# Feed-forward products of a diffusion trunk: which accumulators share a PSUM tile, when the sums of u are formed, and when the conditioning products run

## The chip, the cores and the metric

The kernel runs on one core of a Trainium2 chip. Five engines work from their own in-order instruction queues: PE (TensorE, matrix products into PSUM), DVE (VectorE), ACT (ScalarE), POOL (GpSimd) and SP (SyncE, which here only issues DMAs). An instruction that needs another engine's result waits on a semaphore, and everything behind it in the same queue waits with it. The metric is the device time of one execution in microseconds (us).

## The reference, cut to what matters

There are 512 latent tokens and 256 context tokens, 1024 features wide, in 6 tiles of 128 tokens. Two layers each do a half-step SwiGLU, a token mixer (differential attention in layer 0, grouped-query attention in layer 1) and another half-step SwiGLU; all in float32.

```python
D_MODEL, SEQ, CTX_LEN, DEPTH, N_MOD, D_FF = 1024, 512, 256, 2, 9, 2816

def swiglu(h, w_in, w_out):
    gate, up = jnp.split(h @ w_in, 2, axis=-1)
    return (jax.nn.silu(gate) * up) @ w_out

def adaln(cond, w, b):
    m = jax.nn.silu(cond) @ w + b
    return m.reshape(m.shape[:-1] + (N_MOD, D_MODEL))

def modulated_norm(h, g, m, k):
    return rmsnorm(h, g) * (1.0 + m[..., k + 1, :]) + m[..., k, :]

def half_ffn(h, m, k, g_pre, g_post, w_in, w_out):
    y = swiglu(modulated_norm(h, g_pre, m, k), w_in, w_out)
    return h + 0.5 * m[..., k + 2, :] * rmsnorm(y, g_post)

for i in range(DEPTH):
    ctx_out = i < DEPTH - 1
    m, mc = adaln(c, ada_w[i], ada_b[i]), adaln(c_ctx, ada_w[i], ada_b[i])
    h, hc = (half_ffn(x, mod, 0, g[0], g[1], ffn_w_in[i, 0], ffn_w_out[i, 0]) for x, mod in ((h, m), (hc, mc)))
    ...  # token mixer of the layer; in the last layer the context is only read
    h = half_ffn(h, m, 6, g[4], g[5], ffn_w_in[i, 1], ffn_w_out[i, 1])
    if ctx_out:
        hc = half_ffn(hc, mc, 6, g[4], g[5], ffn_w_in[i, 1], ffn_w_out[i, 1])
```

Each layer has nine modulation vectors v = 0..8 (shift, scale, gate of three sub-layers) for two conditions, that of the latent tokens and that of the context tokens. In the last layer the context tokens are not used after the mixer has read them, so v = 5..8 of layer 1 are wanted for the latent condition alone.

## The kernel before, in words

`trunk` runs six stages one after the other: `ffn` for (layer, half) = (0, 0), `diff_attention`, `ffn` (0, 1), `ffn` (1, 0), `grouped_attention`, `ffn` (1, 1). The first three `ffn` stages work on all six token tiles (384 columns in each of two halves), the last on the four latent tiles (256 columns).

Every float32 operand is split into a rounded high part and a low remainder (`split`, L103 the high part on ACT, L104 the low part on DVE), and a product is three matmuls: high by high, high by low, low by high.

An `ffn` stage has these parts.

* **Direct chunks.** A chunk is 128 columns of `gate` and the same 128 of `up`. Chunk 0 (and chunk 1 in the last stage) is multiplied as it stands, pair of token tiles by pair (`mms`, L459), as soon as a pair's normalised input u is finished (`need`). Where all six tiles are at work, chunk 1 follows as 96 matmuls from L713.
* **Sums of u.** `uh`, `ul` hold u by halves. The kernel then forms four sums of quarters of u, t1, t2, t3 and t4 (L538, L539, L543, L544, L549, L550), in `sums_first` to `sums_fourth`, after the direct chunk 0.
* **Seven-product chunks.** The other 20 chunks use a scheme of Winograd's that needs seven products of half the depth in place of eight (`chunk`, with `product` at L604). Each of the seven products is 12 matmuls. I number them in their order in the queue: 1 (`pa`, g1), 2 (`pc`, s1), 3 (`pb`, s2), 4 (`pd`, s3), 5 (`pa` again, g2), 6 (`pc` again, s4), 7 (`pd` again, u2). `pa` and `pc` are the two banks of one PSUM tile x (`bank2`), `pb` and `pd` are tiles of one bank each.
* **What a chunk does beside PE.** ACT copies `pa` into c1 (L620), `pc` into c5 (L623), applies Silu to `pa` (L633) and to a sum (L637). DVE adds z2 = pb + c1 (L626, the *first add*), z3 = pd + z2 (L629, the *second add*), pc + z2 (L636, the *third add*), pd + z2 (L642) and multiplies (L643). POOL adds z3 + c5 (L630) and multiplies (L640). `keep` stores the chunk's result by DMA.
* **Operands of the next chunk** are made during the chunk (`Operands.steps`): four POOL sums of weight halves (L579 to L582, the *POOL sums*), three high parts on ACT and three low parts on DVE of 1024 columns (gate before the first add, two more after the second add), and one of 512 columns (u2) after the third add.
* **Fillers.** The modulation vectors of later stages are computed in the shadow of this: `ada` loads 512 KB of `ada_w` eight times and DVE multiplies and accumulates it for each of the two conditions (L168, L172, the *acc* instructions); PE then adds over partitions (L188, 16 short matmul records), and DVE adds bias and gain. One `ada` is 10 steps, eight of them with acc instructions. `Fillers.fill` is called twice in a chunk, after the first add (*filler one*) and before the last add L642 (*filler two*), and runs as many steps as are due.
* **Output.** `w_out` multiplies by `ffn_w_out` in groups of chunks given by `GROUPS`, and `w_out_last` finishes the tokens and begins the next stage's input (`Finish`).

In `chunk` the order on PE, DVE, ACT and POOL is the written one (`tc.manual_schedule`); outside, a scheduler sets it by readiness and priority. A writer of a tile waits for the earlier readers of that tile, and the unit is the whole tile: product 2 writes the other bank of x and still waits for the copy of `pa`.

## Time and profile before

| | us |
|---|---|
| median of 3 runs | 2971.38 (2970.94 to 2972.20) |
| profiled execution, its own time | 2967.32 |
| its span | 2965.5 |
| PE busy | 2691.8 (91%) |
| DVE busy | 2194.3 (74%) |
| ACT busy, POOL busy | 1190.7 (40%), 1160.7 (39%) |

The median is 4.06 us above the profiled execution. A row of the timeline gives start, duration, engine, line, operation, what is written and read, and in brackets how long the engine had waited and for what. The mean granted clock of TensorE was 0.975 of full speed.

### The profile page before, as it was taken

How to read it: one execution, taken by the hardware profiler on the slowest of the kernel's cores; microseconds unless marked ns; L12 is line 12 of the kernel's file. 1: busy time of each engine (PE TensorE's matmuls, PEld its weight loads, DVE VectorE, ACT ScalarE, POOL GpSimd, SP SyncE). 2: the span in 40 equal slices, each digit the busy share in tenths (PEclk: the TensorE clock that was granted, in tenths of full speed). 3: DMA queues.
4: the chain of work that ended last, by engine and by line, in shares of the span. 5: the costliest groups of instructions: out<-in, count | busy, mean ns of one | idle time of the engine just before them, and what ended most of it. 6: DMA issues, size and time to landing. Idle time of an engine off the chain costs nothing.

```text
span 2965.5 us, 41112 instructions
## 1 busy us (share of the span) xinstructions
PE 2691.8 (91%) x15472; PEld 2441.9 (82%) x15472; DVE 2194.3 (74%) x2894; ACT 1190.7 (40%) x2427; POOL 1160.7 (39%) x1145
## 2 busy tenths in 40 slices
PE   7888989989999988999999989999998999688898
PEld 5878877878999977888878788888887997677777
DVE  4977878566777787977875678888857778666664
ACT  4322323245666565333342333333414555433342
POOL 1655640044333345655600456564005211465601
PEclk9999999999999989999999999999999999899999
DMA  7344447331101123443473234444734112333362
GB/s 226 113 130 138 143 135 255 122 107 54 44 30 46 50 71 99 137 128 119 137 236 122 96 102 133 146 139 139 239 111 142 44 51 65 100 114 111 111 222 88
DMA packets 302176, 355.33 MB, mean 120 GB/s; under 512 B 15848, under 2 KB 234136, under 8 KB 301976
## 3 DMA queue, kind: packets, MB, share of 16 engines
q1 hardware_dynamic: 301976, 352.69, 37.5%
q8 instruction: 122, 2.00, 0.3%
q14 instruction: 78, 0.64, 0.1%
HBM read 304.10 MB, written 48.55 MB: 119 GB/s over the span
## 4 chain that ended last, share of the span: by engine, by line
PE 61%; DVE 16%; issue 9%; ACT 8%; POOL 4%; DMA 2%; SPq 0%; ACTq 0%; DVEq 0%; POOLq 0%
PE y_ps L404 21%; PE ff_ps L604 15%; PE ff_p L604 9%; PE qkv_ps L755 5%; DVE acc L172 4%; DVE wl L104 3%; PE ff_ps L459 2%; PE S L933 1%; ACT wh L103 1%; PE o_ps L1005 1%; DVE h L363 1%; ACT sil L633 1%; ACT y L250 1%; ACT one L620 1%; DVE t L539 1%
## 5 line engine op out<-in xcount | busy, mean ns | idle before, releaser
L404 PE MATMUL y_ps<-wh,gx 128*128 128x512 f32 x1936 | 606.3, 392 | 9.3 <-ACT wh L103 8.0
L404 PEld LDWEIGHTS y_ps<-wh,gx 128*128 128x128 f32 x1936 | 364.4, 188 | 88.9 <-ACT wh L103 10.1
L604 PE MATMUL ff_ps<-uh,wh 128*128 128x384 f32 (+1 forms) x960 | 323.2, 337 | 102.0 <-ACT sil L633 75.5
L104 DVE TENSOR_TENSOR wl<-stage,wh 128x1024 fp32r<-128x1024 f32 x204 | 309.7, 1521 | 121.7 <-ACT wh L103 121.4
L404 PE MATMUL y_ps<-wl,gx 128*128 128x512 f32 x968 | 379.2, 392 | 2.7 <-DVE wl L104 2.6
L172 DVE SCALAR_TENSOR_TENSOR acc<-stage,scond,acc 128x1024 f32<-128x1024 f32 x224 | 359.1, 1642 | 0.3 <-DMA stage<-in_ada_w 0.3
L395 DVE TENSOR_TENSOR y<-y_ps,y 128x512 f32<-128x512 f32 x324 | 222.2, 687 | 154.5 <-PE y_ps L404 153.7
L103 ACT CAST wh<-stage 128x1024 fp32r<-128x1024 f32 x204 | 211.8, 1052 | 272.8 <-PE y_ps L404 239.5
L604 PE MATMUL ff_ps<-uh,wl 128*128 128x384 f32 (+1 forms) x960 | 314.9, 328 | 4.4 <-DVE wl L104 4.4
L604 PE MATMUL ff_ps<-ul,wh 128*128 128x384 f32 (+1 forms) x960 | 314.1, 327 | 0.0
L604 PE MATMUL ff_p<-t,wh 128*128 128x384 f32 (+1 forms) x1280 | 305.7, 324 | 0.0
L350 POOL TENSOR_TENSOR yg<-y,g 128x512 f32<-128x512 f32 x44 | 59.2, 1346 | 592.7 <-DVE y L395 590.5
L604 PEld LDWEIGHTS ff_ps<-uh,wh 128*128 128x128 f32 x960 | 185.4, 193 | 126.4 <-ACT sil L633 98.7
L630 POOL TENSOR_TENSOR g<-two,one 128x384 f32<-128x384 f32 (+1 forms) x80 | 141.5, 1768 | 313.6 <-issue 108.9
L104 DVE TENSOR_TENSOR wl<-raw,wh 128x1024 fp32r<-128x1024 f32 x160 | 222.6, 1412 | 48.0 <-ACT wh L103 47.9
L604 PEld LDWEIGHTS ff_p<-t,wh 128*128 128x128 f32 x1280 | 225.2, 191 | 3.7 <-issue 3.7
L103 ACT CAST wh<-raw 128x1024 fp32r<-128x1024 f32 x160 | 167.0, 1046 | 149.3 <-POOL raw L582 149.3
L404 PEld LDWEIGHTS y_ps<-wl,gx 128*128 128x128 f32 x968 | 182.6, 189 | 43.8 <-DVE wl L104 7.0
L604 PE MATMUL ff_ps<-t,wh 128*128 128x384 f32 (+1 forms) x640 | 162.5, 339 | 51.3 <-ACT one L620 51.3
L604 PE MATMUL ff_p<-t,wl 128*128 128x384 f32 (+1 forms) x640 | 206.8, 323 | 0.0
L604 PEld LDWEIGHTS ff_ps<-uh,wl 128*128 128x128 f32 x960 | 185.9, 194 | 5.8 <-DVE wl L104 5.8
L604 PEld LDWEIGHTS ff_ps<-ul,wh 128*128 128x128 f32 x960 | 186.0, 194 | 0.0
(237 smaller groups left out, 6518.2 us busy)
## 6 DMA issues: line engine op xcount, KB each, us to landing
stage<-in_ffn_w_in SPq DMA_DIRECT2D x176, 512.0 KB
stage<-in_ada_w SPq DMA_DIRECT2D x136, 512.0 KB
stage<-in_ffn_w_out SPq DMA_DIRECT2D x88, 512.0 KB
gd<-g SPq DMA_DIRECT2D x66, 384.0 KB
gr<-gd SPq DMA_DIRECT2D x60, 384.0 KB
stage<-in_da_w_in SPq DMA_DIRECT2D x64, 192.0 KB
hd<-h SPq DMA_DIRECT2D x18, 512.0 KB
h<-hd SPq DMA_DIRECT2D x16, 512.0 KB
```

Source lines behind the costliest of these rows:

```text
L103: nc.scalar.copy(hi, src)
L104: nc.vector.tensor_tensor(out=lo, in0=src, in1=raw(hi), op=ALU.subtract)
L172: nc.vector.scalar_tensor_tensor(out=acc[c], in0=st, scalar=scond[:, k, c : c + 1], in1=acc[c], op0=ALU.mult, op1=ALU.add)
L250: nc.scalar.activation(junk, src, AF.Square, accum_out=ss)
L350: nc.gpsimd.tensor_tensor(out=self.yg[:, cols], in0=ys[t][:, cols], in1=self.gate[1 if t < CT else 0][:, cols], op=ALU.mult)
L363: nc.vector.scalar_tensor_tensor(out=h, in0=yg, scalar=r, in1=h, op0=ALU.mult, op1=ALU.add)
L395: nc.vector.tensor_tensor(out=y, in0=ps, in1=y, op=ALU.add)
L404: nc.tensor.matmul(ps, lhsT=x, rhs=w, start=(i == 0), stop=(i == n - 1))
L459: nc.tensor.matmul(ps, lhsT=ww[:, k, :], rhs=moving(uu, k, two), start=(k == 0 and n == 0), stop=(k == KC - 1 and n == 2),)
L604: nc.tensor.matmul(ps[:, :hw], lhsT=ww[:, k * P : (k + 1) * P], rhs=bb[:, k, cols], start=(first and k == 0 and n == 0), stop=(last and k ...
L630: nc.gpsimd.tensor_tensor(out=g[:, 1], in0=z3, in1=c5, op=ALU.add)
L755: nc.tensor.matmul(ps[:, :n], lhsT=x, rhs=w, start=(k == 0 and m == 0), stop=(k == KC - 1 and m == 2))
```

## The change

* In `chunk`, `pa` and `pb` now share the two-bank tile, `pc` and `pd` have tiles of their own. Products 1 and 2 so write different tiles, and so do 5 and 6; the tile of products 1, 3 and 5 is read by c1, the first add and the Silu.
* Token tile t lies in half t % 2 at place t // 2 (`full`), so that a pair of tiles is one place in both halves.
* `sum_up` forms t1, t2, t3 for one pair of tiles; in the stages after the first it is called for pair n - 1 once pair n is finished, ahead of pair n's direct products, and for the last pair after the evacuation of chunk 0. t4 follows after chunk 1. The operand steps of the first seven-product chunk begin ahead of the evacuation.
* In the last stage direct chunk 1 has accumulators of its own (`nextp`).
* An `ada` that accumulates on DVE takes 13 steps in place of 10: two empty ones between the last acc and the PE sum, one more before the transposes. `Fillers.total` follows.
* Vectors 5 to 8 of layer 1 are computed for the latent condition alone, and their context gates are not loaded.
* `GROUPS` is (3, 3, 3, 3, 3, 2, 5) in place of (2, 3, 3, 3, 3, 3, 5), and the first group's operands are made one by one in the last chunk's steps; the slots that the operands of `w_out` go round in become "kvvktttt" from "kkttttvv".

```diff
-GROUPS = (2, 3, 3, 3, 3, 3, 5)
+GROUPS = (3, 3, 3, 3, 3, 2, 5)
...
+        conds = range(1 if l and v >= 5 else 2)
...
         if vector:
+            yield
+            yield
             ps = bank("ada_ps")
-            for c in range(2):
+            for c in conds:
...
         yield
+        if vector:
+            yield
...
-            self.total, self.points, self.ran, self.at = (KC + 2) * len(vectors), points, 0, 0
+            self.total, self.points, self.ran, self.at = (KC + (5 if vector else 2)) * len(vectors), points, 0, 0
...
+        def sum_up(two):
+            a1, a2, b1, b2 = quarters(two)
+            nc.vector.tensor_tensor(out=a1, in0=b1, in1=a1, op=ALU.subtract)
+            high_sum(t1, two, a1)
+            nc.gpsimd.tensor_tensor(out=b1, in0=b2, in1=b1, op=ALU.subtract)
+            nc.vector.tensor_tensor(out=b2, in0=b2, in1=a1, op=ALU.subtract)
+            high_sum(t2, two, b2)
+            nc.gpsimd.tensor_tensor(out=a2, in0=a2, in1=b2, op=ALU.subtract)
+            low_sum(t1, two, a1)
+            low_sum(t2, two, b2)
+            high_sum(t3, two, b1)
+            low_sum(t3, two, b1)
...
+            nextp = None if wide else [bank("ff_ps2") for _ in range(2)]
...
             for n, two in enumerate(pairs):
                 for t in two:
                     need(t)
+                if n:
+                    sum_up(pairs[n - 1])
                 for m, (q, x, w) in enumerate(ws):
-                    mms(pss[x][:, column(q, n)], w, two)
+                    mms((nextp if q else pss)[x][:, column(n)], w, two)
...
             x = bank2("ff_ps")
-            pa, pc, pb, pd = x[:, 0], x[:, 1], bank("ff_p6"), bank("ff_p7")
+            pa, pb, pc, pd = x[:, 0], x[:, 1], bank("ff_p5"), bank("ff_p7")
...
+            after = run[0].steps()
+            for _ in range(3):
+                next(after)
             evacuate(0, 0)
...
-            sums_first()
-            after = run[0].steps()
-            next(after)
-            sums_second()
-            next(after)
-            sums_third()
+            for two in pairs if opening else pairs[-1:]:
+                sum_up(two)
             for _ in after:
                 pass
             evacuate(1, 1)
-            sums_fourth()
...
-    full = {0: (0, 0), 1: (1, 0), 2: (0, 1), 3: (0, 2), 4: (1, 1), 5: (1, 2)}
+    full = {t: (t % 2, t // 2) for t in allt}
```

Three places of the program, as the engines' queues have them before and after.

PE, second seven-product chunk of stage (0, 0), the seam of products 1 and 2. `ff_ps` is the tile x, `ff_p_966` a tile of one bank, `t` a sum of u. Before:

```order
L604 MATMUL ff_ps<-uh,wh 128x384
L604 MATMUL ff_ps<-ul,wh 128x384
L604 MATMUL ff_ps<-uh,wl 128x384
L604 MATMUL ff_ps<-t,wh 128x384 [waits Activation_49]
L604 MATMUL ff_ps<-t,wh 128x384
L604 MATMUL ff_ps<-t,wl 128x384 [waits DVE_49]
```

and after:

```order
L597 MATMUL ff_ps<-uh,wh 128x384
L597 MATMUL ff_ps<-ul,wh 128x384
L597 MATMUL ff_ps<-uh,wl 128x384
L597 MATMUL ff_p_966<-t,wh 128x384 [waits Activation_49]
L597 MATMUL ff_p_966<-t,wh 128x384
L597 MATMUL ff_p_966<-t,wl 128x384 [waits DVE_49]
```

Product 2 has moved out of the tile that the copy of `pa` reads; what it still waits for on ACT is the high part of its own weights.

PE, the same chunk, the seam of products 4 and 5. Before:

```order
L604 MATMUL ff_p_967<-t,wh 128x384 x2
L604 MATMUL ff_p_967<-t,wl 128x384
L604 MATMUL ff_ps<-uh,wh 128x384 [waits Activation_49]
L604 MATMUL ff_ps<-ul,wh 128x384
L604 MATMUL ff_ps<-uh,wl 128x384
```

and after:

```order
L597 MATMUL ff_p_967<-t,wh 128x384 x2
L597 MATMUL ff_p_967<-t,wl 128x384
L597 MATMUL ff_ps<-uh,wh 128x384 [waits DVE_49]
L597 MATMUL ff_ps<-ul,wh 128x384
L597 MATMUL ff_ps<-uh,wl 128x384
```

Product 5 waited for ACT (the copies c1 and c5) and now waits for DVE (the first add, which reads `pb` in the same tile).

DVE, the same chunk, from the low part of the gate weights to the last multiplication. `two<-...,one` is the first add, `two<-...,two` the second. Before:

```order
L104 TENSOR_TENSOR wl<-stage,wh 128x1024
L626 TENSOR_TENSOR two<-ff_p_966,one 128x384
L172 SCALAR_TENSOR_TENSOR acc<-stage,scond,acc 128x1024 x2
L629 TENSOR_TENSOR two<-ff_p_967,two 128x384
L104 TENSOR_TENSOR wl<-raw,wh 128x1024 x2
L636 TENSOR_TENSOR sil<-ff_ps,two 128x384
L104 TENSOR_TENSOR u_1079<-stage,u_1078 128x512
L172 SCALAR_TENSOR_TENSOR acc<-stage,scond,acc 128x1024 x2
L642 TENSOR_TENSOR g<-ff_p_967,two 128x384
L643 TENSOR_TENSOR g<-g,sil 128x384
```

and after:

```order
L104 TENSOR_TENSOR wl<-stage,wh 128x1024
L619 TENSOR_TENSOR two<-ff_ps,one 128x384
L173 SCALAR_TENSOR_TENSOR acc<-stage,scond,acc 128x1024 x4
L622 TENSOR_TENSOR two<-ff_p_967,two 128x384
L104 TENSOR_TENSOR wl<-raw,wh 128x1024 x2
L629 TENSOR_TENSOR sil<-ff_p_966,two 128x384
L104 TENSOR_TENSOR u_1083<-stage,u_1082 128x512
L173 SCALAR_TENSOR_TENSOR acc<-stage,scond,acc 128x1024 x2
L635 TENSOR_TENSOR g<-ff_p_967,two 128x384
L636 TENSOR_TENSOR g<-g,sil 128x384
```

Filler one of this chunk has four acc instructions in place of two: with 13 steps to a vector, more steps are due at each call, and those with acc instructions come closer together.

## Rows read from the trace of the kernel before

**Rows 1.** The page's first line.

```profile
span 2965.5 us, 41112 instructions
```

**Rows 2.** Busy time by stretches, each from the first copy c1 to the twentieth, in stages (0, 0), (0, 1), (1, 0), (1, 1): stretch, its length, then busy time (instructions) of PE, PEld, DVE, ACT, POOL, then granted clock, DMA share, GB/s.

```profile
94.55:438.71 344.16, 301.96 (x1664) 283.79 (x1664) 280.61 (x256) 102.44 (x153) 192.14 (x114) 0.96 0.45 136
1171.62:1487.00 315.38, 291.21 (x1648) 276.51 (x1648) 256.36 (x233) 102.80 (x154) 188.46 (x114) 1.00 0.42 130
1747.24:2064.54 317.30, 291.56 (x1648) 276.32 (x1648) 273.05 (x243) 102.92 (x154) 192.18 (x114) 1.00 0.45 139
2570.90:2824.63 253.73, 211.38 (x1596) 203.06 (x1596) 176.52 (x188) 93.72 (x152) 156.81 (x114) 0.95 0.38 115
```

**Rows 3.** Who waited for whom, PE alone: engine, line waited at, releaser: us in total, times, longest.

```profile
PE ff_ps L604 <- ACT sil L633: 75.5, 80, 5.1
PE ff_ps L604 <- ACT one L620: 51.3, 80, 1.2
PE ff_ps L604 <- ACT sil L512: 16.5, 1, 16.5
PE ada_ps L188 <- DVE acc L172: 11.9, 3, 6.0
PE ff_ps L604 <- ACT wh L103: 10.1, 3, 4.1
```

**Rows 4.** Timeline of PE and ACT in one chunk of stage (0, 1): first and last matmul of product 5, then the Silu of `pa` that follows it.

```profile
1343.99 0.33 PE L604 MATMUL ff_ps<-uh,wh 128*128 128x384 f32 x1
1345.90 0.34 PE L604 MATMUL ff_ps<-uh,wl 128*128 128x384 f32 x1
1346.28 0.49 ACT L633 ACTIVATE sil<-ff_ps 128x384 f32<-128x384 f32 x1 [2.06 <-PE ff_ps L604]
```

**Rows 5.** Timeline of ACT in the same stage: the copies c1 of two neighbouring chunks, then a copy c5 and a Silu of `pa`.

```profile
1271.86 0.48 ACT L620 COPY one<-ff_ps 128x384 f32<-128x384 f32 x1 [2.59 <-PE ff_ps L604]
1274.78 0.48 ACT L623 COPY one<-ff_ps 128x384 f32<-128x384 f32 x1 [2.44 <-PE ff_ps L604]
...
1281.02 0.49 ACT L633 ACTIVATE sil<-ff_ps 128x384 f32<-128x384 f32 x1 [3.86 <-PE ff_ps L604]
...
1288.17 0.48 ACT L620 COPY one<-ff_ps 128x384 f32<-128x384 f32 x1 [2.59 <-PE ff_ps L604]
```

**Rows 6.** Timeline of DVE in the same stage. First the end of a chunk with acc instructions in filler two and the head of the next; then, after the dots, a chunk without: low part of the gate weights, a later low part, third add, low part of u2, acc instructions of a new vector.

```profile
1252.87 4.53 DVE L172 SCALAR_TENSOR_TENSOR acc<-stage,scond,acc 128x1024 f32<-128x1024 f32 x2
1257.32 0.55 DVE L642 TENSOR_TENSOR g<-ff_p,two 128x384 f32<-128x384 f32 x1
...
1258.89 2.29 DVE L104 TENSOR_TENSOR wl<-stage,wh 128x1024 fp32r<-128x1024 f32 x1
1261.11 0.55 DVE L626 TENSOR_TENSOR two<-ff_p,one 128x384 f32<-128x384 f32 x1
...
1276.24 1.22 DVE L104 TENSOR_TENSOR wl<-stage,wh 128x1024 fp32r<-128x1024 f32 x1 [4.21 <-ACT wh L103]
...
1282.48 1.23 DVE L104 TENSOR_TENSOR wl<-raw,wh 128x1024 fp32r<-128x1024 f32 x1 [1.85 <-ACT wh L103]
1283.95 0.56 DVE L636 TENSOR_TENSOR sil<-ff_ps,two 128x384 f32<-128x384 f32 x1 [0.25 <-PE ff_ps L604]
1285.61 1.16 DVE L104 TENSOR_TENSOR u<-stage,u 128x512 fp32r<-128x512 f32 x1 [1.10 <-ACT u L103]
1286.70 3.47 DVE L168 TENSOR_SCALAR acc<-stage,scond 128x1024 f32<-128x1024 f32 x2
```

**Rows 7.** Timeline of DVE in the same stage, the acc instructions of one filler one.

```profile
1344.61 2.47 DVE L172 SCALAR_TENSOR_TENSOR acc<-stage,scond,acc 128x1024 f32<-128x1024 f32 x2
```

**Rows 8.** Timeline of POOL in the same stage: the last of the four POOL sums of one chunk, while DVE runs the rows of 1257.32 to 1258.89 above, and that of the next chunk, while DVE waits ahead of the row of 1276.24.

```profile
1258.52 1.59 POOL L582 TENSOR_TENSOR raw<-stage,raw 128x512 f32<-128x512 f32 x1
...
1274.38 1.29 POOL L582 TENSOR_TENSOR raw<-stage,raw 128x512 f32<-128x512 f32 x1
```

**Rows 9.** The PE sums of `ada`: one of them in the timeline of PE, then, after the dots, their busy time in the first three stretches of Rows 2 (stretch, its length, PE and PEld with instructions, clock, DMA share, GB/s; 16 records belong to one vector). In the fourth stretch there is none.

```profile
156.63 2.28 PE L188 MATMUL ada_ps<-acc,pick 128*32 128x256 f32 x16 [5.95 <-DVE acc L172]
...
94.55:438.71 344.16, 6.64 (x64) 1.73 (x64) 0.96 0.45 136
1171.62:1487.00 315.38, 3.21 (x48) 1.25 (x48) 1.00 0.42 130
1747.24:2064.54 317.30, 3.55 (x48) 1.05 (x48) 1.00 0.45 139
```

**Rows 10.** Timeline of stage (1, 1): DVE's low part of the gate weights in one chunk, then, after the dots, first and last matmul of a later product on PE.

```profile
2641.80 2.34 DVE L104 TENSOR_TENSOR wl<-stage,wh 128x1024 fp32r<-128x1024 f32 x1 [2.40 <-ACT wh L103]
...
2648.79 0.28 PE L604 MATMUL ff_ps<-uh,wh 128*128 128x256 f32 x1
...
2650.11 0.28 PE L604 MATMUL ff_ps<-uh,wl 128*128 128x256 f32 x1
```

**Rows 11.** Timeline of the seam between direct and seven-product chunks: in stage (1, 1) the Silu of the second direct chunk on ACT; then in stage (0, 1) two of the sums of u on DVE.

```profile
2567.24 0.58 ACT L512 ACTIVATE sil<-ff_ps 128x512 f32<-128x512 f32 x1
...
1149.00 1.23 DVE L539 TENSOR_TENSOR t<-y,t 128x512 fp32r<-128x512 f32 x1 [0.69 <-ACT t L538]
...
1155.26 1.78 DVE L549 TENSOR_TENSOR y<-y,y 128x512 f32<-128x512 f32 x1
```

**Rows 12.** Timeline of POOL in stage (0, 0): a POOL sum that waited for its weights.

```profile
224.76 2.03 POOL L579 TENSOR_TENSOR raw<-stage 128x512 f32<-128x512 f32 x1 [4.46 <-DMA stage<-in_ffn_w_in]
```

More of the change, by code (lines that the diff above doesn't have):

```diff
@@ L160, in ada @@
         s, what = divmod(v, 3)
+        conds = range(1 if l and v >= 5 else 2)
         ps = None if vector else bank("ada_ps")
-        acc = [ep.tile([P, D], F32, tag="e", name="acc", bufs=3) for _ in range(2)] if vector else None
+        acc = [ep.tile([P, D], F32, tag="e", name="acc", bufs=3) for _ in conds] if vector else None
         for k in range(KC):
@@ L165, in ada @@
             nc.sync.dma_start(out=st, in_=a["ada_w"][l, k * P : (k + 1) * P, v * D : (v + 1) * D])
-            for c in range(2) if vector else ():
+            for c in conds if vector else ():
                 if k == 0:
@@ L220, in ada @@
             gd = dr.tile([2, D], F32, name=f"gd{l}{v}", tag=f"gd{l}{v}")
-            for c in range(2):
+            for c in conds:
                 nc.sync.dma_start(
@@ L443, in moving @@
         def moving(x, k, two):
-            if place[two[0]][1] == 0:
-                return x[:, :, k, 0:P]
-            return x[:, place[two[0]][0], k, P:HALF]
+            j = place[two[0]][1]
+            return x[:, :, k, j * P : (j + 1) * P]
         def keep(c, g):
@@ L692, in opened @@
         def opened():
-            yield
-            yield
-            yield
-            yield
-            ops.append(operand(0))
-            yield
-            ops.extend(operand(c) for c in range(1, GROUPS[0]))
+            for c in range(GROUPS[0]):
+                yield
+                ops.append(operand(c))
             yield
@@ L728, in ffn @@
             evacuate(1, 1)
-            sums_fourth()
+            for two in pairs:
+                high_sum(t4, two, quarters(two)[1])
+            for two in pairs:
+                low_sum(t4, two, quarters(two)[1])
             for n, now in enumerate(run):
```

90 lines of the change are left out of this document (32 added, 58 removed).

## The prediction

> **What bounds the kernel now.** I read the page's engine shares first, then the waits of PE, then busy time by stretches, and last the timelines of single chunks. PE is busy for 91% of a span of 2965.5 us [rows 1], so only its gaps and its own instructions can give time back. The list of PE's waits [rows 3] names the gaps: 75.5 us in 80 waits for the Silu of `pa`, 51.3 us in 80 waits for the copy c1, and one of 16.5 us in the last stage. The first two come once in each of the 80 seven-product chunks, and both are false in part: products 2 and 6 write the other bank of the tile that c1 and Silu read. Those chunks fill four stretches [rows 2], first c1 to twentieth, that is 19 periods each: 344.2, 315.4, 317.3 and 253.7 us, 1230.6 in all.
>
> What a period could be: product 5 runs from 1343.99 to 1345.90 in 11 steps [rows 4], 0.1736 us a matmul, so a product is 2.08 and the seven of a chunk 14.58. In the last stage 2648.79 to 2650.11 [rows 10] gives 0.12 a matmul, 1.44 a product, 10.08 a chunk. A chunk that nothing else disturbs takes 16.31 (from one c1 at 1271.86 to the next at 1288.17 [rows 5]), the two waits on top of the floor.
>
> **The change part by part.**
>
> **The accumulators.** By the order of PE, product 2 no longer waits for c1 and product 6 no longer for Silu. In their place product 5 waits for the first add, which reads `pb`, now in product 5's tile, and product 7 for the second add. The second add stood behind nothing PE wanted before; now the whole DVE queue up to it is on PE's path: the low part of the gate weights, and for product 7 filler one too. The question is whether the first add is done 4 products (8.33) after a chunk's start. I walk it through for each kind of chunk.
>
> *Light chunk (no acc instructions late in the one before).* Product 2 ends at 4.17. A reader on ACT starts 0.21 behind the end of a product (last start 1345.90 + 0.17 against the Silu at 1346.28 [rows 4]), so c5 starts at 4.38. From c5 to the low gate part it is 1.46 (1274.78 [rows 5] to 1276.24 [rows 6]), then 1.22 for it and 0.55 for the add: done at 7.6, before 8.33. The period is the floor; I take 14.7 to 14.8, for short restarts.
>
> *Two acc instructions in filler two.* These run into the next chunk's first add, and a loop closes over DVE, from one first add's end to the next: product 5 (0.05 + 2.08), Silu's start 0.21, from there to the low part that follows it 1.46 (1281.02 [rows 5] to 1282.48 [rows 6]), 1.22 for that, 1.66 from the third add to the low part of u2 (1283.95 to 1285.61), 1.09 to filler two (1286.70), 4.45 for the two acc (1252.87 to 1257.32), 1.57 to the low gate part (1258.89), 2.22 for that, and 0.55 [all in rows 6]. The sum is 16.56, more than 14.58 and no better than the 16.31 of before. What makes it long are rows beside POOL: the acc pair takes 4.53 there and 2.47 where POOL doesn't run beside it [rows 7], the low part 2.29 in place of 1.22 while POOL's last sum stretches from 1.29 to 1.59 [rows 8]. With the durations of the undisturbed rows the loop is 16.56 - 2.06 - 1.07 = 13.4, below the floor. The bounds of such a chunk are therefore 14.6 and 16.6. I take 16.6, since both disturbed rows come from just this place in the chunk, and POOL's sums are not moved.
> The page "SBUF — State Buffer" of the Trainium skill (section "SBUF: two separate sides") says that VectorE, with two operands in SBUF, and GpSimd hold a shared port by an exclusive lock for a whole instruction, and the other is fully blocked; the disturbed rows agree. By that rule the loop stays at 16.6 as long as POOL has its turns there; without it the time would be that of the first rival below.
>
> *Four acc instructions in filler one and two in filler two.* An `ada` of 13 steps makes the steps come in bursts (third place in the order). From the first add's end: four acc 4.94 (twice 2.47), second add 0.55, two low parts 2.44, and the rest of the loop from the third add on, 1.66 + 1.09 + 4.45 + 1.57 + 2.22 + 0.55 = 11.54. The sum is 19.5: product 5 is 3.4 late and product 7 another 1.4. A chunk with few acc instructions behind such a one still pays the 3.4: 18.0.
>
> *Last stage.* Light throughout after the change: one acc in filler one of every other chunk, none in filler two. Product 2 ends at 2.88, c5 at 3.09, low gate part at 4.55, beside POOL it takes 2.34 [rows 10], the shorter add about 0.37 (0.55 by 256 to 384 columns): 7.3 against a due time of 5.76, so 1.5 late. The period is 11.6, with bounds of 10.5 (low part undisturbed, 1.22) and 12.
>
> **The sum over the stretches**, with the kinds counted from DVE's order after the change. `ada`'s sums over partitions are PE's own work, 2.28 a vector [rows 9], four, three, three and no vectors in the stretches before and after alike.
> (0, 0): 8 x 14.8 + 9 x 19.5 + 2 x 18.0 + 9 = 339, against 344.2: -5.
> (0, 1): 12 x 16.6 + 7 x 14.7 + 7 = 309, against 315.4: -6.
> (1, 0): 13 x 14.8 + 2 x 19.5 + 3 x 18.0 + 16.6 + 7 = 309, against 317.3: -8.
> (1, 1): 19 x 11.6 = 220, against 253.7: -33.
> Together -52.
>
> **The seams.** In the last stage direct chunk 1 gets tiles of its own, and the 16.5 us at the head of product 1 [rows 3], which end with the Silu at 2567.24 [rows 11], go. Late next is the last pair's u, and the first chunk's first add behind the last sums; these give back some 5: -11. In the other three the operands of the first chunk begin ahead of the evacuation, and the 10.1 us of waits for their high parts [rows 3] go, with some waits for low parts beside them. But the sums of u for pair n - 1 stand in DVE's queue ahead of pair n + 1's normalisation. Such a sum takes 1.23 and 1.78 [rows 11]; three of the one and one of the other are 5.5 us, less what DVE idles there, so some 4 us a stage are given back: -3 together. The two empty steps ahead of PE's sums over partitions are to end the 11.9 us of waits for acc [rows 3]; those lie in the stretches and are covered by the kinds of chunk above. For restarts of PE behind the stalls that stay I add 4. Seams: -10.
>
> **Costed at nothing.** The 32 acc instructions dropped for the context condition in layer 1 and the loads of its gates: DVE is not the bound in the chunks where they fall out, once the last stage's kind above is counted; if it were, 32 x 1.24 = 40 us of DVE would come on top. `GROUPS`, the slots of `w_out`'s operands and the even and odd places move work beside PE's products; a miss would cost a wait of one or two us at six group heads.
>
> **Sum.** -52 - 10 = -62 against the profiled execution's 2967.3 us: 2905. The median of the runs stands 4.1 above that execution, so 2909.
>
> **The rivals.**
> **(a) PE becomes the only bound.** The DVE loop doesn't close, since POOL's sums finish before the acc instructions come when PE no longer waits in between. Then 14.6 for every chunk without a burst, 17 with one (four acc beside 2.5 us of slack), 10.6 in the last stage: 9 x 17 + 10 x 14.6 + 9 = 308, 19 x 14.6 + 7 = 284, 2 x 17 + 17 x 14.6 + 7 = 289, 19 x 10.6 = 201: -148, and seams -10: 2809 in the profile, 2813. For it: rows 7, and that POOL is idle for 45% of the first stretch (192.1 of 344.2 busy [rows 2]). Against: both disturbed rows.
> **(b) Little is left.** Light chunks too meet POOL at the low gate part (7.6 + 1.07 = 8.7, 0.35 late, 28 times: +10), bursts take 21 (+16), the last stage 12.2 (+11), the seams bring nothing (+10): 2956.
> **(c) Slower, by the bursts' loads.** A chunk with six acc instructions wants three 512 KB loads of `ada_w` besides its own weights, through the same four staging slots. POOL already waited 4.46 us for weights to land once [rows 12]. If a slot comes free only when the burst has read it, the next chunk's sums start late, and a burst chunk takes 24, the one after it 21: (0, 0) 9 x 24 + 2 x 21 + 118 + 9 = 385 (+41), (1, 0) +14, (0, 1) +8, the last stage -22, the seams 0: +41, so 3012. It decides once a burst chunk takes more than about 22. For it: bursts in nearly half of the chunks of (0, 0). Against: DMA is busy for only 0.45 of that stretch [rows 2].
> **(d) The change doesn't do what it says**, and another reader holds product 2 or 6: no change, 2971. PE's order shows no such wait.
>
> **How the numbers follow.** My forecast has 0.57, (a) 0.20, (b) 0.12, (c) 0.09, (d) 0.02. Between (a) and the forecast lie mixed cases, in which some stages close the loop and others don't; the range reaches three quarters of the way to (a) and on the other side to (b): 2840 to 2958. What a measurement of this kernel can tell from no change is 0.2%, some 6 us. Faster takes the forecast, (a) and most of (b): 0.86; same (d) and the edge of (b): 0.04; slower (c) and what lies beyond (b): 0.10.
>
> **What would show it.** In the profile after: no waits at products 2 and 6 for ACT; in their place product 5 waits for the first add, L619, on DVE, about 2 us in chunks behind acc instructions in filler two, 3 to 5 in bursts, 1.5 in the last stage. Periods of c1 of 14.6 to 14.8, 16.6, 18 to 19.5 and 11.6 by kind. The wait of 16.5 us gone. Acc instructions beside POOL at 4.5 a pair in filler two. The forecast is wrong if chunks with two acc in filler two run at 14.6 (a), or if bursts pass 22 with POOL waiting for DMA (c).

## The result, and the profile after

The changed kernel takes 2886.66 us (2886.29 to 2886.81), the kernel before beside it 2971.16: a ratio of 0.9715, interval 0.9699 to 0.9732, 84.5 us faster. Its profiled execution has a span of 2884.8 us, 80.7 less than that of before. The forecast was 2909 us, 62 less than before, in a range of 2840 to 2958.

First the four stretches of the changed kernel, from the first copy c1 to the twentieth, with the columns of [rows 2].

```profile
92.88:421.48 328.60, 296.50 (x1658) 287.18 (x1657) 270.11 (x257) 102.85 (x154) 194.80 (x113) 0.96 0.48 145
1146.64:1460.78 314.14, 289.92 (x1648) 283.45 (x1647) 247.35 (x226) 102.82 (x153) 179.65 (x110) 0.98 0.42 127
1716.97:2021.28 304.31, 286.46 (x1642) 280.75 (x1641) 240.61 (x225) 102.97 (x152) 184.04 (x110) 0.99 0.48 145
2513.01:2747.27 234.26, 199.88 (x1600) 194.46 (x1599) 167.85 (x182) 90.42 (x153) 157.14 (x113) 0.99 0.42 126
```

| stretch | before | after | change | forecast change |
|---|---|---|---|---|
| (0, 0) | 344.2 | 328.6 | -15.6 | -5 |
| (0, 1) | 315.4 | 314.1 | -1.2 | -6 |
| (1, 0) | 317.3 | 304.3 | -13.0 | -8 |
| (1, 1) | 253.7 | 234.3 | -19.5 | -33 |
| all four | 1230.6 | 1181.3 | -49.3 | -52 |
| ahead of the first c1 | | | -12.9 | -14 |
| behind the last c1 | | | -18.6 | 0, and +4 for restarts |

The last two lines are worked out from the starts of c1 and of each stage's first direct matmul in the timelines; with the stretches they make up the 80.7 us of the span. That the sum of the stretches came out as forecast is luck: errors of 5 to 14 us of both signs met.

Of the 49.3 us, 26 are idle time of PE (length less PE busy, 134.5 before and 108.5 after) and 23 are PE's own busy time, 1096.1 before and 1072.8 after (3 of them in the sums of `ada`). Half of these 23 lie in the last stage: 211.4 and 199.9, at a granted clock of 0.95 and 0.99. So a stall costs PE more than its idle time; the windows below show how.

PE's waits after, as in [rows 3], with one line of another kind, the transposition of a token's normalised tile (`pre_t`):

```profile
PE ff_ps L597 <- DVE two L619: 95.8, 50, 3.6
PE pre_t L268 <- DVE y L377: 23.7, 11, 8.7
PE ff_p L597 <- DVE two L622: 7.7, 7, 2.4
PE ff_ps L597 <- ACT one L613: 4.9, 7, 0.7
PE y_ps L412 <- DVE wl L104: 1.3, 2, 0.8
PE y_ps L412 <- ACT wh L103: 1.1, 2, 0.5
```

and the lines of before that answer to them and are not in [rows 3]:

```profile
PE pre_t L263 <- DVE y L369: 14.9, 12, 2.5
PE y_ps L404 <- ACT wh L103: 8.0, 5, 3.6
```

The 80 waits for the Silu and nearly all of the 80 for c1 are gone, and with them the 16.5 us in the last stage and the 11.9 us for acc. In their place product 5 waits for the first add in 50 of the 80 chunks, 95.8 us, and product 7 for the second add in seven: 126.8 us of waits have become some 108.

**A chunk in which the loop closes.** Timeline of the changed kernel in stage (0, 1), from one first add (L619) to the next; the row of PE at the end is the first matmul of product 5.

```profile
1168.49 0.55 DVE L619 TENSOR_TENSOR two<-ff_ps,one 128x384 f32<-128x384 f32 x1
...
1171.82 3.17 DVE L104 TENSOR_TENSOR wl<-raw,wh 128x1024 fp32r<-128x1024 f32 x2
1174.91 0.55 DVE L629 TENSOR_TENSOR sil<-ff_p,two 128x384 f32<-128x384 f32 x1
1176.56 1.16 DVE L104 TENSOR_TENSOR u<-stage,u 128x512 fp32r<-128x512 f32 x1 [1.10 <-ACT u L103]
1177.64 4.55 DVE L173 SCALAR_TENSOR_TENSOR acc<-stage,scond,acc 128x1024 f32<-128x1024 f32 x2
...
1181.06 2.28 POOL L574 TENSOR_TENSOR raw<-stage 128x512 f32<-128x512 f32 x1
1183.31 1.58 POOL L575 TENSOR_TENSOR raw<-stage,raw 128x512 f32<-128x512 f32 x1
1183.68 2.28 DVE L104 TENSOR_TENSOR wl<-stage,wh 128x1024 fp32r<-128x1024 f32 x1
...
1185.89 0.55 DVE L619 TENSOR_TENSOR two<-ff_ps,one 128x384 f32<-128x384 f32 x1
...
1186.49 0.69 PE L597 MATMUL ff_ps<-uh,wh 128*128 128x384 f32 x1 [2.54 <-DVE two L619]
```

From one first add to the next it is 17.4 us, DVE idle for only 1.1 of them. The acc pair and the low gate part are as long as in [rows 6], 4.55 and 2.28, with POOL's sums beside them.

**What a stall costs beyond itself.** The same place in windows: stretch, its length, PE busy (records), granted clock, DMA share, GB/s. The first is the wait of 2.54 us, the next two follow it; the fourth follows a wait of 1.76 us for the same releaser one chunk later, and the last another wait of 2.54 us.

```profile
1183.90:1186.49 2.59, 0.05 (x2) 0.89 0.81 317
1186.49:1189.50 3.01, 3.01 (x10) 0.53 0.62 176
1189.50:1192.50 3.00, 3.00 (x19) 1.00 0.60 175
1204.38:1208.00 3.62, 3.62 (x21) 1.00 0.54 155
1221.80:1224.80 3.00, 3.00 (x17) 1.00 0.63 181
```

After the first 2.54 us PE runs for 3 us at 0.53 of its full clock on average, mostly at the lower of its two levels (1.2 GHz), and the next matmuls start 0.32 us apart instead of 0.17. So this chunk took 18.7 us from c1 to c1: 14.6, the wait, and some 1.5 more. Behind the 1.76 us the clock was 1.00. The length of a stall alone does not decide it: stage (0, 1) has six stalls of 2.54 us, and behind four of them the clock of the next 3 us was 0.50 to 0.72 (chunks of 18.7 to 19.0 us), behind the other two 1.00 (chunks of 17.4 us). In number 11 a stall of 1.33 us was followed by 3 us at 0.50. What decides it is open.

**The last stage.** Timeline of POOL, ACT and DVE over two chunks of the changed kernel, the first with an acc in filler one, the second without.

```profile
2568.88 1.96 DVE L173 SCALAR_TENSOR_TENSOR acc<-stage,scond,acc 128x1024 f32<-128x1024 f32 x1
2569.71 2.27 POOL L575 TENSOR_TENSOR raw<-stage,raw 128x512 f32<-128x512 f32 x1
2572.02 1.05 ACT L103 CAST wh<-raw 128x1024 fp32r<-128x1024 f32 x1 [6.03 <-POOL raw L575]
2573.11 2.44 DVE L104 TENSOR_TENSOR wl<-raw,wh 128x1024 fp32r<-128x1024 f32 x2 [1.94 <-ACT wh L103]
2575.47 0.42 DVE L629 TENSOR_TENSOR sil<-ff_p,two 128x256 f32<-128x256 f32 x1
2575.92 0.42 ACT L630 ACTIVATE sil<-sil 128x256 f32<-128x256 f32 x1 [1.63 <-DVE sil L629]
2576.47 0.72 POOL L633 TENSOR_TENSOR g<-g,sil 128x256 f32<-128x256 f32 x1 [3.79 <-ACT sil L630]
2577.16 1.75 POOL L572 TENSOR_TENSOR raw<-stage 128x512 f32<-128x512 f32 x1
...
2582.52 1.29 POOL L575 TENSOR_TENSOR raw<-stage,raw 128x512 f32<-128x512 f32 x1
```

From the second row on, each row ends just ahead of the next one's start, on three engines in turn: last POOL sum, cast of r1, low parts, third add, Silu, POOL's multiplication, and behind it in POOL's queue the four sums for the next chunk. That is a closed chain of its own: its rows from 2569.71 + 2.27 to 2582.52 + 1.29 make 11.8, the period of the stage's light chunks. Where an acc runs beside the last sum, that sum takes 2.27 instead of 1.29 and the period is 12.8.

### The profile page after: what moved, and what is told of

Same layout as the page of the kernel before. It is cut to its first block, busy times and chain, and to the rows that moved or that the text cites. A ratio compares the mean times of both kernels' runs of the same rounds, so it can differ in the third digit from the quotient of the medians.

```text
span 2884.8 us, 41039 instructions
## 1 busy us (share of the span) xinstructions
PE 2664.4 (92%) x15440; PEld 2452.4 (85%) x15440; DVE 2128.7 (74%) x2866; ACT 1186.5 (41%) x2431; POOL 1160.9 (40%) x1145
## 5 line engine op out<-in xcount | busy, mean ns | idle before, releaser
L104 DVE TENSOR_TENSOR wl<-stage,wh 128x1024 fp32r<-128x1024 f32 x204 | 315.8, 1553 | 90.1 <-ACT wh L103 89.7
L173 DVE SCALAR_TENSOR_TENSOR acc<-stage,scond,acc 128x1024 f32<-128x1024 f32 x196 | 310.6, 1623 | 2.3 <-DMA stage<-in_ada_w 2.1
L597 PE MATMUL ff_ps<-uh,wh 128*128 128x384 f32 (+1 forms) x640 | 219.6, 343 | 95.9 <-DVE two L619 95.8
L104 DVE TENSOR_TENSOR wl<-raw,wh 128x1024 fp32r<-128x1024 f32 x160 | 204.9, 1293 | 95.5 <-ACT wh L103 95.3
L623 POOL TENSOR_TENSOR g<-two,one 128x384 f32<-128x384 f32 (+1 forms) x80 | 141.5, 1769 | 285.5 <-issue 206.8
L597 PEld LDWEIGHTS ff_ps<-uh,wh 128*128 128x128 f32 x640 | 126.2, 197 | 110.6 <-DVE two L619 110.0
L597 PE MATMUL ff_ps<-ul,wh 128*128 128x384 f32 (+1 forms) x640 | 213.2, 333 | 0.0
L597 PE MATMUL ff_ps<-uh,wl 128*128 128x384 f32 (+1 forms) x640 | 213.0, 333 | 0.0
L597 PE MATMUL ff_p<-uh,u 128*128 128x384 f32 (+1 forms) x640 | 165.8, 325 | 7.7 <-DVE two L622 7.7
L633 POOL TENSOR_TENSOR g<-g,sil 128x384 f32<-128x384 f32 (+1 forms) x80 | 76.4, 955 | 228.6 <-ACT sil L630 226.1
L597 PE MATMUL ff_ps<-t,wh 128*128 128x384 f32 (+1 forms) x640 | 152.2, 322 | 4.9 <-ACT one L613 4.9
```

Source lines behind the costliest of these rows:

```text
L104: nc.vector.tensor_tensor(out=lo, in0=src, in1=raw(hi), op=ALU.subtract)
L173: nc.vector.scalar_tensor_tensor(out=acc[c], in0=st, scalar=scond[:, k, c : c + 1], in1=acc[c], op0=ALU.mult, op1=ALU.add)
L597: nc.tensor.matmul(ps[:, :hw], lhsT=ww[:, k * P : (k + 1) * P], rhs=bb[:, k, cols], start=(first and k == 0 and n == 0), stop=(last and k ...
L623: nc.gpsimd.tensor_tensor(out=g[:, 1], in0=z3, in1=c5, op=ALU.add)
L633: nc.gpsimd.tensor_tensor(out=g[:, 1], in0=g[:, 1], in1=sil[:, 1], op=ALU.mult)
```

## The experiments

Each is an edit of the changed kernel unless said otherwise, timed beside the kernel before; times are medians, and periods are differences of the starts of c1.

**1. The old pairing of accumulators.**

```diff
-            pa, pb, pc, pd = x[:, 0], x[:, 1], bank("ff_p5"), bank("ff_p7")
+            pa, pc, pb, pd = x[:, 0], x[:, 1], bank("ff_p6"), bank("ff_p7")
```

> The changed kernel with one thing undone: the accumulators are paired as before (pa with pc in the two-bank tile). Theory A (the new pairing is what shortened the chunks): products 2 and 6 wait for c1 and the Silu again, 1.6 us in every chunk, and the four stretches go back towards those of before: some 80 x 1.5 = 120 us of waits come back, less the 96 us of waits for the first add that go, so about 2910. Theory B (the pairing alone gives little: what it removes, product 5's wait for the first add takes back wherever acc instructions run, and the shorter stretches come from where the acc instructions fall): chunks of 16.3 in the three wide stages whatever the bursts, 11.6 in the last: stretches of about 319, 317, 317 and 221, 1174 against 1181, so 2875 to 2885.

Measured: 2923.55 us (ratio 0.9832, 0.9818 to 0.9847), 37 more than the changed kernel. Stretches 334.5, 319.3, 319.8, 238.8. The false waits are back:

```profile
PE ff_ps L597 <- ACT sil L626: 62.5, 77, 2.1
PE ff_ps L597 <- ACT one L613: 52.0, 80, 3.7
```

Theory A, with a time 14 us above its own. Theory B falls: light chunks are at 16.4, but bursts still take 17 to 20, so the old pairing is no shelter from them, and the new one is worth 37 us in the changed kernel. In the last stage it is worth little: 15 of the 19.5 us that stretch (1, 1) gained are there with the old pairing too.

**2. The new pairing alone, in the kernel before.** The same line, the other way round.

> The kernel before with one thing done: pa and pb share the two-bank tile, pc and pd have their own. Nothing else is changed: 10 steps a vector, sums of u after the direct chunk. Theory A: chunks drop to 14.6 where no acc instructions stand in filler two and to 16.6 at most where they do; most chunks of the wide stages have two in each filler, so -30 at most there, and the last stage goes to 12 or so (-25): 2915 to 2930. Theory B: chunks with two and two stay at 16.6 to 17.4 (+0.3 to +1 each), the stalls at the end of each vector stay, the last stage gains some 20: 2950 to 2970.

Measured: 2949.66 (0.992, 0.9906 to 0.9935), 23 less than before, at the edge of theory B and outside A. Periods of 14.6 appear behind chunks without acc instructions in filler two, mostly 16.6 to 19 behind those with two there, and up to 24.5 where a vector ends and PE's sums still stand right behind the last acc. Its main wait:

```profile
PE ff_ps L604 <- DVE two L626: 117.1, 59, 5.9
```

The pairing alone is worth 23 us, and 37 among the other parts. Where the difference lies is seen in the last nine periods of stage (1, 0), where the change drops the context condition's acc instructions. The rows give these periods in the kernel before, in number 1, in this run and in the changed kernel: stretch, its length, busy time (count) of the acc instructions on DVE, granted clock, DMA share, GB/s.

```profile
1916.46:2064.54 148.08, 45.34 (x28) 1.00 0.46 140
1902.22:2050.47 148.25, 25.54 (x16) 1.00 0.47 146
1907.08:2055.10 148.02, 45.04 (x29) 0.98 0.46 140
1886.57:2021.28 134.71, 28.93 (x16) 1.00 0.53 161
```

Dropping them, with the rest of the change, under the old pairing gives nothing (second row), the new pairing with all of them gives nothing (third row), and both together give 13.4 us: all that stretch (1, 0) gained, and nearly all of the 14 us between the two prices.

**3. The first add ahead of the low gate part.**

```diff
-            next(after, None)
             product(pb, now.s2, t2, True, True)
             add(out=z2, in0=pb[:, :hw], in1=c1)
+            next(after, None)
             fillers.fill()
```

> The changed kernel with one thing moved: on DVE the first add stands ahead of the low part of the gate weights instead of behind it. Theory A (a loop from first add to first add decides, and everything in DVE's queue ahead of it is part of it): the low part, 1.2 to 2.3 us, leaves the loop: 16.6 becomes 14.4, below the floor of 14.58; a burst becomes 17.2; the last stage 10.1 to 10.5. Stretches of about 310, 290, 292 and 199 against 329, 314, 304 and 234: -90, so 2795 to 2815. Theory B (DVE's load as such decides, whatever stands first): what product 5 no longer waits, product 7 waits for the second add; less than 25 us are gained: 2860 to 2887.

Measured: 2856.44 (0.9605, 0.9589 to 0.9621), 30 less than the changed kernel, between the theories. Stretches 322.8, 301.2, 295.6, 232.2.

```profile
PE ff_p L597 <- DVE two L622: 37.9, 24, 4.2
PE ff_ps L597 <- ACT one L613: 23.8, 18, 1.3
PE ff_ps L597 <- DVE two L618: 22.8, 17, 1.9
```

The wait for the first add falls from 95.8 to 22.8, and 37.9 come up at product 7 for the second add, as B says of the rest. The waits for c1 are nearly all in the last stage (22.5 us in its stretch), where the periods stay at 11.8 and 12.8: the first add wasn't what set them.

**4. Ten steps to a vector.** The three empty `yield` of an accumulating `ada` taken out, and `Fillers.total` with them.

> The changed kernel with the three empty steps of each ada taken out again (10 steps a vector). Theory A (bursts of four and two acc instructions cost, 19.2 us a chunk against 16.6 for two and two): fewer bursts, -10 to -15 in stages (0, 0) and (1, 0); but PE's sums stand right behind the last acc again and stall some 12 us as before: 2880 to 2890. Theory B (the empty steps are a gain, because a stall of PE at an ada sum also breaks the run of the chunk): the waits ada_ps<-acc come back with 12 us or more and stretch (0, 0) has chunks of 24: 2895 to 2910.

Measured: 2887.22 (0.9708, 0.9694 to 0.9723), the same as the changed kernel. Stretches 335.0, 311.7, 300.1, 238.3. The time is theory A's, its gain in (0, 0) is not: that stretch grew by 6.4. Both effects are there and cancel: periods of 23.2 and 23.5 come back in (0, 0) where a vector ends, and 10.8 us of waits of PE's sums for acc, while (0, 1) and (1, 0) are 2 to 4 shorter with fewer bursts. Stretch (1, 1) is 4 longer.

**5. POOL reads nothing for its sums.**

```diff
-                nc.gpsimd.tensor_tensor(out=r1[:, left], in0=up[:, left], in1=up[:, right], op=ALU.add)
-                sub(out=r2[:, left], in0=r1[:, left], in1=gate[:, left])
-                sub(out=r2[:, right], in0=gate[:, left], in1=up[:, left])
-                sub(out=r1[:, right], in0=gate[:, right], in1=r2[:, left])
+                nc.gpsimd.memset(r1[:, left], 0.01)
+                nc.gpsimd.memset(r2[:, left], 0.01)
+                nc.gpsimd.memset(r2[:, right], 0.01)
+                nc.gpsimd.memset(r1[:, right], 0.01)
```

> The changed kernel with the four POOL sums of a chunk replaced by fills with a constant of the same shape: POOL still writes those tiles but reads nothing for them. It leaves out the sums of weight halves, so the products are of other numbers; only the time counts. Theory A (DVE and POOL shut each other out, and that is what makes the loop over the first add longer than the floor): acc pairs in filler two take 2.5 us instead of 4.5, the gate's low part 1.2 instead of 2.3; chunks with two and two acc at 14.6 to 15, bursts at 17, the last stage at 10.1 to 10.8: stretches of about 300, 284, 288 and 203 against 329, 314, 304 and 234, so 2775 to 2800. Theory B (those instructions are long for another reason, their DMA or their own operands, and the loop is DVE's own work): durations stay, 2865 to 2887.

Measured: 2743.57 (0.9236, 0.9222 to 0.9249). Stretches 286.1, 280.5, 281.2, 198.3; two and two at 14.6, bursts mostly at 15.0 to 15.3, the last stage mostly at 10.5. That is 31 us below theory A's range. PE is busy for 1040.7 us of the 1046.1 in the four stretches, at a clock of 1.00 in each. The groups of acc instructions by line and form (count | busy, mean ns | idle before), first of the changed kernel:

```profile
L173 DVE SCALAR_TENSOR_TENSOR acc<-stage,scond,acc 128x1024 f32<-128x1024 f32 x196 | 310.6, 1623 | 2.3 <-DMA stage<-in_ada_w 2.1
```

then of this one, followed by an acc pair in its timeline and a fill that runs beside it:

```profile
L173 DVE SCALAR_TENSOR_TENSOR acc<-stage,scond,acc 128x1024 f32<-128x1024 f32 x196 | 242.7, 1277 | 2.5 <-DMA stage<-in_ada_w 2.3
...
1139.91 2.47 DVE L173 SCALAR_TENSOR_TENSOR acc<-stage,scond,acc 128x1024 f32<-128x1024 f32 x2
1140.31 0.53 POOL L573 MEMSET raw<- 128x512 f32 x1
```

Theory A: an acc is 1.28 us on average, in place of 1.62, and none of 2.3 is left (the longest takes 1.53). That fills are short is not the reason: the 59 acc instructions that run beside a fill take 1.27 us on average, the 135 that run beside nothing of POOL 1.28. The page "SBUF — State Buffer" of the Trainium skill (section "SBUF: two separate sides") names just this condition, that the lock holds against a GpSimd instruction that reads SBUF; the trace agrees. The 143 us by which this kernel is faster are no clean price of that, since a fill is 0.53 us long where a sum is 1.3 to 2.3, which shortens POOL's chain of the last stage by itself.

**6. POOL's multiplication behind the next sums.** In `chunk`, the multiplication L633 and `keep` are put off until the next chunk's sums are issued.

```diff
             next(after, None)
+            while late:
+                late.pop(0)()
...
-            nc.gpsimd.tensor_tensor(out=g[:, 1], in0=g[:, 1], in1=sil[:, 1], op=ALU.mult)
...
-            keep(now.c, g.rearrange("p i n -> p (i n)"))
+            late.append(finish)
```

> The changed kernel with one thing moved: POOL's multiplication of a chunk (L633) and the DMA of its result stand behind the POOL sums that follow instead of ahead of them. Theory A (in the last stage a loop over POOL sets the 11.8: multiplication, four sums, cast of r1, low parts, third add, Silu, multiplication again; the first add is late for the same reason or hardly matters): the sums no longer wait for the Silu of the third add, the last stage's chunks fall to 10.8 to 11.5, stretch 234 to 210-220, the wide stages lose nothing: 2865 to 2877. Theory B (my forecast's reason: the low gate part beside POOL makes the first add 1.5 late): stretch (1, 1) stays at 230 or more, 2880 to 2890.

Measured: 2876.33 (0.9685, 0.967 to 0.9699), 10 less. Stretch (1, 1) is 228.6, chunks mostly between 10.5 and 13.5. Below 11.8 at times, so POOL's chain was a limit, but not the only one. The time lies in theory A's range, but its reason is half there: the last stage gives 5.7 us instead of 14 to 24, and stretch (0, 1) gives 8. The others are 330.1, 306.1 and 306.0. What stands in the way shows in POOL's waits for weights: 12.7 us in stretch (1, 1), where the changed kernel has none, and 103.5 against 21.6 in all. Numbers 8 and 12 follow that up.

**7. Nothing in filler two's place.** First add, low gate part, second add, both fillers, and the low part of u2 at the end of the chunk.

```diff
-            next(after, None)
             product(pb, now.s2, t2, True, True)
             add(out=z2, in0=pb[:, :hw], in1=c1)
-            fillers.fill()
+            next(after, None)
             product(pd, now.s3, t3, True, False)
             add(out=z3, in0=pd[:, :hw], in1=z2)
+            fillers.fill()
+            fillers.fill()
...
             nc.scalar.activation(sil[:, 1], sil[:, 1], AF.Silu)
-            next(after, None)
-            fillers.fill()
```

> The changed kernel with DVE's order in a chunk rearranged: first add, low gate part, second add, then both fillers, and the low part of u2 at the chunk's end; nothing in filler two's place. Theory A (acc instructions cost twice in filler two because POOL's sums run there, and the adds stand behind what PE doesn't want): acc pairs at 2.5 us, chunks with four acc in all at 14.6 to 15, bursts 16, the last stage still 11.8 by POOL's loop: stretches of about 295, 285, 287 and 225, so 2790 to 2810. Theory B (DVE's load decides; moving it shifts the waits): as with the first add alone, 2840 to 2860.

Measured: 2853.27 (0.9607, 0.9591 to 0.9621): theory B. Stretches 321.8, 294.5, 295.6, 232.3. Four acc in a row make the low parts late (28.1 us of waits of PE for L104 in 26 chunks), and an acc still takes 1.56 us on average: 44 of them now run beside POOL's addition L623 (1.86 on average) and 40 beside the last POOL sum (2.03).

**8. Numbers 6 and 7 together.**

> The two edits before this one together: DVE's order rearranged, and POOL's multiplication behind the next sums. Theory A: they add, since they open different loops: wide stages 14.6 to 15, last stage 10.3 to 10.8 (stretch 200): 2765 to 2785. Theory B (one loop stands behind both): the better of the two alone, no more.

Measured: 2905.97 (0.9787, 0.9769 to 0.9806), worse than either and than the changed kernel; neither theory. SP's queue shows why, in the waits of its DMA issues; L457 is `keep`:

```profile
SPq L457 <- POOL g L642: 434.6, 76, 8.8
```

In the waits of DVE and POOL, `ada_w` and the weights come late, with 2.1 and 21.6 us in the changed kernel:

```profile
DVE acc L173 <- DMA stage<-in_ada_w: 62.1, 23, 6.3
POOL raw L572 <- DMA stage<-in_ffn_w_in: 301.2, 55, 17.4
```

The store of a chunk's result waits for the late multiplication, and the loads of `ada_w` and of weights stand behind it in SP's queue. This is my rival (c), loads too late for the acc instructions, in another kernel.

**9. The old `GROUPS`,** slots and operand steps of `w_out`.

```diff
-GROUPS = (3, 3, 3, 3, 3, 2, 5)
+GROUPS = (2, 3, 3, 3, 3, 3, 5)
-        slots = cycle("kvvktttt")
+        slots = cycle("kkttttvv")
...
```

> The changed kernel with GROUPS, the slots of w_out's operands and the making of the first group's operands as before. Between the last copy c1 of a stage and the next stage the changed kernel is 18.6 us shorter over the four stages, which I had put at nothing. Theory A (it is this part of the change): 2897 to 2907. Theory B (it comes from the chunk that stands ahead of it and from w_out's matmuls moving into the last chunk's stalls): 2883 to 2891.

Measured: 2894.78 (0.9746, 0.9732 to 0.9761), 8.1 more than the changed kernel, between the two. The stretches are unchanged (327.7, 314.1, 303.8, 234.2).

**10. Sums of u after the direct chunk.**

```diff
-                if n:
-                    sum_up(pairs[n - 1])
...
-            for two in pairs if opening else pairs[-1:]:
+            for two in pairs:
```

> The changed kernel with the sums of u formed after the direct chunk again, all pairs in a row (still pair by pair, t4 last). Theory A (sums as the pairs come take DVE work out of the way of the first seven-product chunk): the first chunk waits for t1 and t2, some 10 us in the last stage and 0 to 3 in the others: 2893 to 2902. Theory B (my forecast's view: they delay u by 4 us a stage and give that back behind it, so that undoing costs little): 2880 to 2890.

Measured: 2882.76 (0.97, 0.9684 to 0.9716): no difference from the changed kernel that the intervals show, theory B. The first periods of (0, 1) and (1, 0) grow from 14.6 to 17.9, while the wait for `pre_t` falls from 23.7 to 20.1: only 3.6 of the 8.8 us by which it rose with the change.

**11. Both adds first, both fillers kept.** The edit of number 3, and:

```diff
+            product(pd, now.s3, t3, True, False)
+            add(out=z3, in0=pd[:, :hw], in1=z2)
             fillers.fill()
-            product(pd, now.s3, t3, True, False)
-            add(out=z3, in0=pd[:, :hw], in1=z2)
...
             nc.scalar.activation(sil[:, 1], sil[:, 1], AF.Silu)
-            next(after, None)
             fillers.fill()
```

(the step for u2 then runs at the chunk's end).

> The changed kernel with the first add ahead of the low gate part, the second add ahead of filler one, and the low part of u2 behind the last multiplication; both fillers stay. Against the run with the first add alone (2856). Theory A (product 7's 38 us of waits for the second add go, and the 1.1 us in which DVE waits for the cast of u2 in each chunk): two and two at 15.5 to 15.9, bursts at 18, stretches of about 308, 294, 289, 231: 2835 to 2848. Theory B (DVE is full in these chunks, waits only move, to the low parts as in the run with one filler): 2850 to 2860.

Measured: 2819.11 (0.9488, 0.9474 to 0.9502), the fastest with the whole computation in it: 68 less than the changed kernel, and 16 below theory A's range. Its stretches, as above:

```profile
93.91:401.53 307.62, 289.29 (x1668) 278.02 (x1666) 271.91 (x257) 100.16 (x153) 180.19 (x113) 1.00 0.51 154
1130.59:1415.58 284.99, 282.09 (x1648) 277.76 (x1647) 240.06 (x226) 101.20 (x153) 177.44 (x110) 1.00 0.46 140
1671.10:1959.46 288.36, 282.57 (x1642) 277.62 (x1641) 234.77 (x227) 101.59 (x153) 168.35 (x110) 1.00 0.51 153
2447.35:2679.36 232.01, 203.11 (x1604) 195.91 (x1602) 155.86 (x184) 89.36 (x153) 156.58 (x113) 0.99 0.44 128
```

Two and two now take 14.6 to 15.6, bursts up to 18.0, and the granted clock is 1.00 in the three wide stages. PE waits 16.4 us for the first add in all, and the last stage stays at 11.8 and 12.8.

**12. Number 11, with POOL's multiplication late in the last stage alone.**

> The run before with POOL's multiplication behind the next sums in the last stage alone, where there is only one acc in every other chunk. Theory A (in the last stage two loops of 11.6 to 11.8 stand side by side, over the first add and over POOL, so that each edit alone gave little there; both together open it): stretch (1, 1) 200 to 210 in place of 232, so 20 to 30 less than the run before. Theory B (a third limit, the stores or loads that SP has behind the store of a chunk, or DVE and POOL beside each other): stretch 222 or more, within 10 of the run before.

Measured: 2835.16 (0.9545, 0.953 to 0.956), 16 more than number 11; stretch (1, 1) is 245.3, the others are as there. Theory B, and its third limit shows in one row of POOL, the first sum of a chunk:

```profile
2511.76 1.35 POOL L572 TENSOR_TENSOR raw<-stage 128x512 f32<-128x512 f32 x1 [4.69 <-DMA stage<-in_ffn_w_in]
```

with SP ahead of it:

```profile
SPq L457 <- POOL g L644: 119.6, 20, 7.7
```

As in number 8, the late store holds up the next weights in SP's queue. The row of stretch (1, 1), to be read against the last one of number 11, shows where the time goes:

```profile
2447.69:2692.97 245.28, 213.39 (x1604) 209.32 (x1602) 162.47 (x184) 91.41 (x154) 155.89 (x113) 0.92 0.41 121
```

Of the 13.3 us that the stretch is longer, only 3 are idle time of PE; 10.3 are PE busy time, at a granted clock of 0.92 instead of 0.99. The stalls are fewer but up to 3.3 us long instead of 1.3 to 1.4. The store on a queue of its own was not tried.

## Why the prediction was right, and where it was not

* **The accumulators.** Right in mechanism: the waits at products 2 and 6 went, product 5 waits for the first add in the chunks behind acc instructions, and those chunks don't gain. Numbers 1 and 2 price the pairing at 37 and 23 us; the forecast expected 52 from the chunks. Numbers 3 and 11 show that the queue ahead of the two adds is what PE waits for.
* **The light chunk:** 14.6 to 14.8, as worked out.
* **Two acc in filler two:** the term was too small. I had 16.6; in (0, 1) the chunks behind such a one took 15.5 to 19.0, 17.4 on average, hence -1.2 there instead of -6. Two things were missing: the two low parts stretch to 3.17 us when POOL's addition L623 runs beside them (17.4 a loop), and behind four of the six longest stalls came a lower clock, some 1.5 us each.
* **Restarts:** I had 4 us for them, and in the seams. PE is busy for 1072.8 us in the four stretches and for 1040.7 in number 5, where it hardly stalls: some 30 us for slow matmuls behind stalls, in the chunks themselves.
* **Bursts:** 17.8 to 19.9 where one follows another, as the 19.5 says, but 14.6 to 18.5 where it follows another kind or opens the stage: its lateness falls on the next chunk, and I charged it twice. The nine bursts of (0, 0) took 17.9 on average, and the stretch came out at -15.6 instead of -5.
* **PE's sums:** I took the 2.28 of the one row in the timeline for each vector. [Rows 9] themselves have 1.66, 1.07 and 1.18 on average in the three stretches; after the change it was 1.07 in the first two. Of the 9, 7 and 7 us in the forecast's sums, some 4 each should not have been there.
* **The last stage:** 234 instead of 220, with light chunks near the forecast (11.8 against 11.6) for another reason. I had the first add beside POOL as the limit. Number 3 takes that away and the period doesn't move; the chain over POOL's queue sets it, and number 6, which opens that chain, finds the weights late. An acc in filler one, which I counted as nothing, costs 1 us through POOL's last sum, in seven chunks, and the first period took 15.2. Most of the gain of this stage is not the pairing's (number 1); it comes with the rest of the change, in which half as many acc instructions run there, a part that no run undoes alone.
* **The seams:** ahead of the chunks -12.9 against -14, with the 16.5 us gone as forecast; the sums of u by pairs neither gain nor lose (number 10). The wait for `pre_t` rises by 8.8, near the 4 a stage, but number 10 puts only 3.6 of that down to the sums.
* **"Costed at nothing"** was wrong in two places. Behind the last c1 of a stage I had no gain, and it was 18.6, by far the largest miss. To the end of the last chunk 4.0 are gained: about 7.7 by the pairing (numbers 2 and 9 both have that), less 3.8 for the first group's operands, which are now made there. Behind that end 14.6 are gained: 11.0 by `GROUPS` and these operands, as number 9 shows, and 3.6 whose cause is open. And the dropped acc instructions were not without worth: with the new pairing they are the 13 us of (1, 0) (number 2).
* **The rivals.** (a), PE alone as the bound, is not what happened, though number 5 shows that it would with POOL's reads away, and number 11 nears it in three stages by order alone. (b) had the last stage right: 12.2 a chunk, 12.3 measured. (c) didn't happen: DVE waits 2.1 us for `ada_w` in all; numbers 8 and 12 show the mechanism where a store stands ahead of the loads. (d) falls with the waits at products 2 and 6.

## What to carry to other kernels

A false wait that is removed uncovers the next reader of the same tile, so look at what stands ahead of that reader in its own queue, and reorder there as part of the same change: here the order of two adds and a low part (number 11) was worth 68 us more, the pairing 37. Two parts of a change can be worth nothing singly and 13 us together, so try each with and without the other. A chain that closes over several engines can be found by following rows whose start is another's end, all the way round; taking a step that is only near it out of the way left the period of the last stage at 11.8 (number 3). A store that waits for its data holds up the loads behind it in the same issue queue (numbers 8 and 12).

## What was not expected of the hardware

* Of six stalls of PE of 2.54 us, four were followed by 3 us at a granted clock of 0.50 to 0.72 and two by a clock of 1.00; one of 1.33 us in another run was followed by 0.50. So the idle time of a stall is not its whole price, and its length doesn't tell the rest.
* The acc instruction took 1.28 us on average with POOL filling constants and 1.62 with POOL adding, with the same data and order on DVE; beside a fill it was as short as alone.
* POOL's sum of 128x512 took 1.29 us alone and 2.27 beside an acc: the price of the meeting is paid on both engines, and in the last stage it was POOL's share that set the time.
